# A gate projection moved from behind the first recurrent head to behind all four heads and the rotary key

## The chip, the cores and the metric

One core of a Trainium2 chip runs the whole kernel as one launch. The metric is the device time of one execution in microseconds (us), lower is better. Engines: TensorE (PE, with its weight loads PEld), VectorE (DVE), ScalarE (ACT), GpSimd (POOL), and SyncE (SP), whose queue issues most of the loads.

## The reference, cut to what matters

One transformer-like layer over 512 latent tokens and 256 context tokens, width 1024, all in float32. One input projection feeds multi-head latent attention (4 heads) and a bidirectional gated linear recurrence (HGRN2, 4 heads, 2 directions). The recurrence's output of a head is normalised over its 128 values, scaled, and multiplied by the SiLU of a gate projection `hg`:

```python
    def hgrn_out(o, hg, n):
        o = rmsnorm(o, g_on).astype(hg.dtype).reshape(B, n, HGRN_HEADS * HGRN_VAL_DIM)
        return o * jax.nn.silu(hg)

    lat_out = jnp.concatenate([o_mla_lat, hgrn_out(o_h_lat, hg_l, N)], axis=-1) @ w_out
```

The concatenated head outputs go through `w_out`, a residual with a modulation vector, a second norm, a SwiGLU feed-forward of 2816 columns, and a final norm.

## The kernel before, in words

Every float32 product is split into a high and a low part, and `mm3` (lines 148 to 152) issues three matmuls for it. A weight unit (128x1024) comes in by a load on SP's queue into a `wf` buffer (3 of them), is cast to its high part on ACT (line 132), and its low part is made on DVE (line 133); `wh` and `wl` have 3 buffers each, and `unit(i)` prepares two units ahead. The units are used in the order in which `wi` was packed on the host.

PSUM has two tiles `big` (two banks each) and four tiles `sm` (a bank each).

The order of the stage that the change touches:

- `mla_pass` makes the low-rank query and key inputs, and `mods(6)` and `mods(2)` issue eight `late_mod` sums (line 427: one load of 512 KB and one DVE pass over 128x1024 with a running sum; 32 such sums make the late modulation vectors).
- For each head h: `hgrn_q(h)`, `gates(h, 0)`, `gates(h, 1)`, three projections into a `big` each. After head 0 comes `hg_pass`, the gate projection: it holds both `big` tiles for four units of 24 matmuls, and makes `shg`, the SiLU of the gate, with ACT and DVE (lines 644, 645); between its units it calls `mods(3)`, up to a limit of 12.
- `mla_kpe` projects the rotary key into a `big`, rotates it on DVE, and writes `krh` and `krl`, four ACT casts and four DVE subtractions (lines 726, 727).
- `make_v` (three), `make_qr` (two), `make_q` (four), `make_k(0)`: the attention's values, rotary queries, queries and first keys; then `scores` and the attention (lines 855 to 918); then `wout` (the output projection) with further `mods` in front of it.

The recurrence runs beside this, in generators on the list `side`. `tick()` moves the first three of them on by one step; `project` calls it once or twice in its middle and the main loop calls it after each projection, so that the recurrence's small matmuls stand between projections. `hgrn_dir(h, d)` makes one direction of one head (scan and reciprocal on DVE, transposes, masked scores `pa`, key-value products `kv`, the chain of states `U`). `hgrn_out(h)` waits for both directions and for the gate (`"hg" in done`), sums the two masked score tiles on POOL, makes the head's output in `po` (an `sm`), its norm, the product with `shg` (line 621, four DVE instructions), four transposes (line 627), and `onh`, `onl` (lines 629, 630). For the last head the norm's root is taken with an ACT square root (`fast=last`), and an Exp activation follows it (line 617) so that ACT has Exp's table before the attention. The order on each engine is fixed when the program is built, by a planner that goes by priorities (program order, moved by `prio`) and by its own estimate of when operands are ready.

Of the kernel before, what the change touches and what calls it, by code (L numbers as in the profile page):

```python
# [52 lines left out]
def block_kernel(ctx: ExitStack, tc: tile.TileContext, xT, ctxT, vec, cin, cst, msk, wm, wmt, wi, wqkv, wo, wgu, wd, out):  # L53
# [8 lines left out]
    def nm(s):  # L62
        uid[0] += 1
        return f"{s}_{uid[0]}"
# [4 lines left out]
    def sm():  # L69
        return psum.tile([P, 512], F32, tag="sm", name=nm("sm"), bufs=4)  # L70
# [73 lines left out]
    def unit(i, ahead=2):  # L144
        prefetch(i + 1 + ahead)
        return made[i]
# [320 lines left out]
    HU = 8  # L467

    def gates(h, d):
        ps = project(HU + 3 * h + 1 + d + (4 if h else 0))  # L470
        sg = HG.tile([P, NT], F32, tag="sg", name=nm("sg"), bufs=2)
        nc.scalar.activation(sg, ps[:, :NT], AF.Sigmoid)
        kk = HG.tile([P, NT], F32, tag="kk", name=nm("kk"), bufs=3)
        nc.scalar.activation(kk, ps[:, :NT], AF.Sigmoid, scale=-1.0)
        return sg, kk

    def hgrn_q(h):
        ps = project(HU + 3 * h + (4 if h else 0), ctx_=False)
        q = HG.tile([P, NL], F32, tag="q", name=nm("q"), bufs=2)
        nc.scalar.copy(q, ps[:, :NL])  # L480
        return q
# [106 lines left out]
        dirs[h, d] = (qg, U)  # L588

    def hgrn_out(h):  # L590
        while (h, 0) not in dirs or (h, 1) not in dirs or "hg" not in done:
            yield
        a2 = HG.tile([P, 4, P], F32, tag="a2", name=nm("a2"), bufs=1)
        nc.gpsimd.tensor_add(a2, am[0], am[1])
        for _ in range(3 if h % 2 else 1):
            yield
        po = sm()
        for j in range(4):
            t = po[:, j * P : (j + 1) * P]
            nc.tensor.matmul(t, a2[:, j, :], vt[:, j, h * P : (h + 1) * P], start=True, stop=False,  # L600
                             skip_group_check=True)
            for d in range(2):
                qg, U = dirs[h, d]
                for g in range(2):
                    c = 2 * j + g
                    nc.tensor.matmul(t[g * CH : (g + 1) * CH, :], qg[:, c, :], U[:, c, :], start=False,  # L606
                                     stop=(g == 1 and d == 1), skip_group_check=True, tile_position=(0, g * CH))
        done.add(h)
        sq = HG.tile([P, P], F32, tag="st", name=nm("osq"), bufs=1)
        ss = HG.tile([P, 4], F32, tag="rs_s", name=nm("oss"), bufs=1)  # L610
        for j in range(4):
            nc.scalar.activation(sq, po[:, j * P : (j + 1) * P], AF.Square, accum_out=ss[:, j : j + 1])
        last = h == NH - 1
        with prio(200 if last else 0):
            rr, _ = rstd_cols(HG, (ss, 4), P, fast=last)
        if last:
            nc.scalar.activation(epst2, rr[:, 0:1], AF.Exp, scale=0.0)
        w = HG.tile([P, 4, P], F32, tag="rs_d", name=nm("ow"), bufs=1)
        with prio(200 if last else 0):
            for j in range(4):  # L620
                nc.vector.scalar_tensor_tensor(w[:, j, :], po[:, j * P : (j + 1) * P], rr[:, j : j + 1],
                                               shg[:, j, h * P : (h + 1) * P], op0=ALU.mult, op1=ALU.mult)
        for _ in range(4):
            yield
        pt = sm()
        for j in range(4):
            nc.tensor.transpose(pt[:, j * P : (j + 1) * P], w[:, j, :], ident)
        gon = V("gon")[:, 0:1]
        nc.scalar.activation(onh[:, h, :], pt, AF.Copy, scale=gon)
        nc.vector.scalar_tensor_tensor(onl[:, h, :], pt, gon, onh[:, h, :].bitcast(F32), op0=ALU.mult,  # L630
                                       op1=ALU.subtract)

    def hg_pass():
        acc = [big(), big()]
        acc = [acc[0][:, 0, :], acc[0][:, 1, :], acc[1][:, 0, :], acc[1][:, 1, :]]
        for u in range(4):
            w = unit(HU + 3 + u)
            for tt in range(4):
                for kk in range(2):
                    k = 2 * u + kk  # L640
                    mm3(acc[tt], (hh[:, k, tt * P : (tt + 1) * P], hl[:, k, tt * P : (tt + 1) * P]),
                        sl(w, lambda t: t[:, kk * 512 : kk * 512 + 512]), k == 0, k == KT - 1)
                if u == 3:
                    nc.scalar.activation(shg[:, tt, :], acc[tt], AF.Sigmoid)
                    nc.vector.tensor_mul(shg[:, tt, :], acc[tt], shg[:, tt, :])
                if tt == 1:
                    tick()
            tick()
            mods(3)
        done.add("hg")  # L650

    def mla_pass():
        acc = [big(), big()]
# [72 lines left out]
                nc.scalar.copy(krh[r, c], src)  # L726
                nc.vector.tensor_sub(krl[r, c], src, krh[0:64, c].bitcast(F32))

    KPU = HU + 16
    nm_ = [0]  # L730
    lim_ = [12]

    def mods(n):
        for _ in range(n):
# [6 lines left out]
    for h in range(NH):  # L741
# [6 lines left out]
        side += [hgrn_dir(h, 1, s1, qd), hgrn_out(h)]  # L748
        tick()
        if h == 0:  # L750
            hg_pass()
            mods(12 - nm_[0])
            nc.sync.dma_start(cs[:, CC["cos"][0] :], cst[:, CC["cos"][0] :])
    mla_kpe()
    tick()
    B.release()

    F1 = pool("F1", "right")
# [406 lines left out]
```

## Time and profile before

| | us |
|---|---|
| median of 3 runs | 794.79 |
| lowest, highest run | 792.61, 794.85 |
| profiled execution | 792.44 |
| its span, first to last instruction | 790.6 |

The profiled execution is the one that all rows come from: 1.84 us of its time lie outside the span, and it is 2.35 us under the median. PE is busy for 767.0 us of the span, DVE for 445.0, ACT for 307.2. A wait is shown with the instruction that waited and the one that released it.

### The profile page before, as it was taken

The page shows a single profiled execution, that of the slowest core. Times are in us where ns is not written, and L with a number is a line of the kernel's source. Part 1 is how long each engine was busy: PE and PEld are TensorE (multiplying, and loading weights), DVE is VectorE, ACT ScalarE, POOL GpSimd, SP SyncE. Part 2 cuts the span into 40 slices and gives each one's busy share as a digit, 9 for nine tenths or more (in the row PEclk, how much of TensorE's full clock was granted, in tenths as well). Part 3 has the DMA queues.
Part 4 walks back from the last instruction along what each step waited for, and adds up shares of the span by engine and source line. Part 5 has one row for each costly group of instructions (what it writes and reads, how often), then busy time and mean ns, then how long its engine had stood idle before and what let it go on. Part 6 is the DMA issues. An engine that isn't in the chain of part 4 may idle for free.

```text
span 790.6 us, 10838 instructions
## 1 busy us (share of the span) xinstructions
PE 767.0 (97%) x4342; PEld 630.8 (80%) x4342; DVE 445.0 (56%) x819; ACT 307.2 (39%) x564; POOL 10.1 (1%) x18
## 2 busy tenths in 40 slices
PE   8899999999999989999999999999999999999995
PEld 7568878788887768888999888888888888888885
DVE  4686569739778988984566434432333233223324
ACT  5344245434554576664344223222322222212211
POOL 0000000000000100000000000000000000000000
PEclk8999999999999999999999999999999999999997
DMA  8924723321110022453503354423232333332303
GB/s 326 396 82 142 238 81 107 133 67 61 48 55 28 28 96 98 133 166 148 160 2 107 107 159 133 149 92 107 80 107 82 104 78 96 93 100 82 111 2 107
DMA packets 26708, 88.78 MB, mean 112 GB/s; under 512 B 2977, under 2 KB 5281, under 8 KB 26530
## 3 DMA queue, kind: packets, MB, share of 16 engines
q1 hardware_dynamic: 25570, 87.04, 33.5%
q10 hardware_dynamic: 1088, 1.05, 0.4%
q8 instruction: 34, 0.56, 0.3%
q14 instruction: 16, 0.13, 0.0%
HBM read 85.97 MB, written 2.10 MB: 111 GB/s over the span
## 4 chain that ended last, share of the span: by engine, by line
PE 86%; DVE 7%; DMA 4%; ACT 2%; issue 1%; SPq 0%; DVEq 0%; ACTq 0%
PE big L150 17%; PE big L151 16%; PE big L152 16%; PE sm L150 9%; PE sm L151 9%; PE sm L152 9%; PE big L861 2%; DMA xc<-in_ctxT_dram 1%; PE sm L606 1%; DMA wm<-in_wm_dram 1%; PE big L862 1%; DMA wms<-in_wm_dram 1%; PE sm L880 1%; DVE U L587 1%; PE sm L600 1%
## 5 line engine op out<-in xcount | busy, mean ns | idle before, releaser
L133 DVE TENSOR_TENSOR wl<-wf,wh 128x1024 fp32r<-128x1024 f32 (+2 forms) x100 | 119.6, 1196 | 184.5 <-ACT wh L132 184.3
L132 ACT CAST wh<-wf 128x1024 fp32r<-128x1024 f32 (+2 forms) x100 | 102.9, 1029 | 279.8 <-PE big L151 167.4
L150 PE MATMUL big<-h2h,wh 128*128 128x512 f32 (+1 forms) x368 | 140.3, 381 | 0.0
L151 PE MATMUL big<-h2l,wh 128*128 128x512 f32 (+1 forms) x368 | 140.0, 381 | 0.0
L152 PE MATMUL big<-h2h,wl 128*128 128x512 f32 (+1 forms) x368 | 140.0, 381 | 0.0
L151 PEld LDWEIGHTS big<-h2l,wh 128*128 128x128 f32 x368 | 69.2, 188 | 14.6
L152 PEld LDWEIGHTS big<-h2h,wl 128*128 128x128 f32 x368 | 69.2, 188 | 14.5
L150 PEld LDWEIGHTS big<-h2h,wh 128*128 128x128 f32 x368 | 69.2, 188 | 14.4
L150 PE MATMUL sm<-ah,wh 128*128 128x512 f32 (+1 forms) x198 | 73.5, 371 | 0.0
L152 PE MATMUL sm<-ah,wl 128*128 128x512 f32 (+1 forms) x198 | 73.4, 371 | 0.0
L151 PE MATMUL sm<-al,wh 128*128 128x512 f32 (+1 forms) x198 | 73.4, 370 | 0.0
L427 DVE SCALAR_TENSOR_TENSOR wl<-wl,cs 128x1024 f32<-128x1024 f32 x32 | 39.0, 1220 | 35.0 <-DMA wl<-in_wmt_dram 35.0
L150 PEld LDWEIGHTS sm<-ah,wh 128*128 128x128 f32 x198 | 37.3, 188 | 7.1
L151 PEld LDWEIGHTS sm<-al,wh 128*128 128x128 f32 x198 | 37.3, 188 | 7.1
L152 PEld LDWEIGHTS sm<-ah,wl 128*128 128x128 f32 x198 | 37.3, 188 | 7.1
L150 PE MATMUL big<-hh,wh 128*128 128x512 f32 x104 | 42.8, 411 | 0.0
L150 PE MATMUL big<-wh,hh 128*128 128x512 f32 x96 | 39.4, 414 | 3.3 <-ACT hh L340 1.9
L151 PE MATMUL big<-hl,wh 128*128 128x512 f32 x104 | 40.9, 394 | 0.0
L152 PE MATMUL big<-hh,wl 128*128 128x512 f32 x104 | 40.9, 393 | 0.0
L151 PE MATMUL big<-wl,hh 128*128 128x512 f32 x96 | 38.2, 400 | 0.0
L152 PE MATMUL big<-wh,hl 128*128 128x512 f32 x96 | 38.1, 399 | 0.0
L508 DVE RECIPROCAL G<-S 128x528 f32<-128x528 f32 x8 | 27.5, 3433 | 0.1
(320 smaller groups left out, 1345.9 us busy)
## 6 DMA issues: line engine op xcount, KB each, us to landing
wf<-in_wgu_dram SPq DMA_DIRECT2D x44, 512.0 KB, 3.4
wl<-in_wmt_dram SPq DMA_DIRECT2D x32, 512.0 KB, 3.5
wf<-in_wi_dram SPq DMA_DIRECT2D x25, 512.0 KB, 4.2
wf<-in_wd_dram SPq DMA_DIRECT2D x16, 512.0 KB, 3.5
wms<-in_wm_dram SPq DMA_DIRECT2D x11, 512.0 KB, 9.6
wf<-in_wo_dram SPq DMA_DIRECT2D x8, 512.0 KB, 3.3
wf<-in_wd_dram SPq DMA_DIRECT2D x8, 384.0 KB, 3.1
wm<-in_wm_dram SPq DMA_DIRECT2D x5, 512.0 KB, 10.2
```

Of the source, the lines that this page charges most:

```text
L132: nc.scalar.copy(hi[:, :w], f[:, :w])
L133: nc.vector.tensor_sub(lo[:, :w], f[:, :w], hi[:, :w].bitcast(F32))
L150: nc.tensor.matmul(o, lh, rh, start=start, stop=False, skip_group_check=True)
L151: nc.tensor.matmul(o, lh, rl, start=False, stop=False, skip_group_check=True)
L152: nc.tensor.matmul(o, ll, rh, start=False, stop=stop, skip_group_check=True)
L427: nc.vector.scalar_tensor_tensor(f, f, 1.0, sc, op0=ALU.mult, op1=ALU.mult, accum_out=acc)
L508: nc.vector.reciprocal(I, S)
L587: nc.vector.scalar_tensor_tensor(U[:, c1, :], U[:, c0, :], er[:, 1, c0 : c0 + 1], U[:, c1, :], op0=ALU.mult, op1=ALU.add)
L600: nc.tensor.matmul(t, a2[:, j, :], vt[:, j, h * P : (h + 1) * P], start=True, stop=False, skip_group_check=True)
L606: nc.tensor.matmul(t[g * CH : (g + 1) * CH, :], qg[:, c, :], U[:, c, :], start=False, stop=(g == 1 and d == 1), skip_group_check=True, til ...
L861: nc.tensor.matmul(ps[:, 0, :], L, R[:, :NL], start=(i == 0), stop=(i == 4), skip_group_check=True)
L862: nc.tensor.matmul(ps[:, 1, :NC], L, R[:, NL:], start=(i == 0), stop=(i == 4), skip_group_check=True)
```

## The change

The gate projection `hg_pass` is called after `mla_kpe` instead of after head 0, and its four weight units are packed last in `wi`. `hgrn_out` no longer waits for the gate: it writes the normalised output into the head's own columns of `vt`, the value tile, which no later instruction of that head reads; half of the four writes go to ACT. The new generators `hgrn_fin`, one per head, are put on `side` after the gate pass: they multiply these columns by the gate, one DVE instruction of 128x512, and make the transposes, `onh` and `onl`. The last head's norm is made like the others (three Newton steps on DVE, no square root), the Exp activation moves to the end of `hg_pass`, and the limit of modulation sums before the attention goes from 12 to 8: four sums move into the `mods` calls of the output projection.

```diff
     def hgrn_out(h):
-        while (h, 0) not in dirs or (h, 1) not in dirs or "hg" not in done:
+        while (h, 0) not in dirs or (h, 1) not in dirs:
             yield
...
-        last = h == NH - 1
-        with prio(200 if last else 0):
-            rr, _ = rstd_cols(HG, (ss, 4), P, fast=last)
-        if last:
-            nc.scalar.activation(epst2, rr[:, 0:1], AF.Exp, scale=0.0)
-        w = HG.tile([P, 4, P], F32, tag="rs_d", name=nm("ow"), bufs=1)
-        with prio(200 if last else 0):
-            for j in range(4):
-                nc.vector.scalar_tensor_tensor(w[:, j, :], po[:, j * P : (j + 1) * P], rr[:, j : j + 1],
-                                               shg[:, j, h * P : (h + 1) * P], op0=ALU.mult, op1=ALU.mult)
-        for _ in range(4):
+        rr, _ = rstd_cols(HG, (ss, 4), P)
+        w = vt[:, 0:4, cols]
+        for j in range(4):
+            if j % 2:
+                nc.scalar.activation(w[:, j, :], po[:, j * P : (j + 1) * P], AF.Copy, scale=rr[:, j : j + 1])
+            else:
+                nc.vector.tensor_scalar(w[:, j, :], po[:, j * P : (j + 1) * P], rr[:, j : j + 1], None, op0=ALU.mult)
+        done.add(("n", h))
+
+    def hgrn_fin(h):
+        while ("n", h) not in done:
+            yield
+        w = vt[:, 0:4, h * P : (h + 1) * P]
+        nc.vector.tensor_mul(w, w, shg[:, :, h * P : (h + 1) * P])
+        for _ in range(2):
             yield
         pt = sm()
         for j in range(4):
...
-            mods(3)
-        done.add("hg")
+        nc.scalar.activation(epst2, shg[:, 3, 0:1], AF.Exp, scale=0.0)
+        side.extend(hgrn_fin(h) for h in range(NH))
...
-    lim_ = [12]
+    lim_ = [8]
...
         if h == 0:
-            hg_pass()
-            mods(12 - nm_[0])
+            mods(8 - nm_[0])
             nc.sync.dma_start(cs[:, CC["cos"][0] :], cst[:, CC["cos"][0] :])
     mla_kpe()
     tick()
+    hg_pass()
     B.release()
```

## Rows read from the trace of the kernel before

**Rows 1.** The page, its first part: busy us (share of span) xinstructions.
```profile
PE 767.0 (97%) x4342; PEld 630.8 (80%) x4342; DVE 445.0 (56%) x819; ACT 307.2 (39%) x564; POOL 10.1 (1%) x18
```
**Rows 2.** Stretches: PE, PEld, DVE, ACT, POOL busy (xcount), PE clock, DMA share, GB/s.
```profile
107.30:156.20 48.90, 48.90 (x332) 40.44 (x330) 39.24 (x60) 23.91 (x49) 1.28 (x1) 1.00 0.36 119
156.20:211.40 55.20, 55.20 (x392) 46.60 (x391) 38.02 (x64) 24.30 (x56) 1.28 (x1) 1.00 0.18 58
263.20:296.20 33.00, 29.17 (x187) 21.22 (x185) 30.62 (x60) 22.77 (x47) 3.57 (x4) 1.00 0.21 72
296.20:350.00 53.80, 52.61 (x310) 45.24 (x309) 49.57 (x97) 34.98 (x71) 0.00 (x0) 1.00 0.38 124
350.00:366.00 16.00, 15.13 (x79) 12.47 (x78) 6.19 (x13) 5.68 (x13) 0.00 (x0) 1.00 0.45 165
```
**Rows 3.** Waits of PE, 100 to 300 us: us in total, times, longest us.
```profile
PE big L150 <- DVE krl L727: 1.7, 1, 1.7
...
PE sm L627 <- DVE ow L621: 1.2, 1, 1.2
PE big L150 <- DVE qnl L783: 1.0, 2, 0.7
PE sm L606 <- DVE U L587: 0.6, 1, 0.6
```
**Rows 4.** Timeline of PE at its longest wait: start, duration, instruction [idle before].
```profile
267.91 0.39 PE L152 MATMUL sm<-cq,wl 128*128 128x512 f32 x1
268.14 0.39 PE L150 MATMUL sm<-cq,wh 128*128 128x512 f32 x1
270.19 0.50 PE L150 MATMUL big<-wh,ck 128*128 128x512 f32 x1 [1.67 <-DVE krl L727]
```
**Rows 5.** The gate pass: its matmuls (one group of three) and its DVE product.
```profile
L150 PE MATMUL big<-wh,hh 128*128 128x512 f32 x32 | 13.2, 412 | 0.0
...
L645 DVE TENSOR_TENSOR shg<-big,shg 128x512 f32<-128x512 f32 x4 | 2.8, 689 | 2.7 <-ACT shg L644 2.7
```
**Rows 6.** DVE's groups from 263.2 to 296.2 us: busy us, mean ns | idle before.
```profile
L133 DVE TENSOR_TENSOR wl<-wf,wh 128x1024 fp32r<-128x1024 f32 x4 | 4.9, 1216 | 0.4 <-ACT wh L132 0.4
L810 DVE TENSOR_TENSOR vl<-big,vh 128x512 fp32r<-128x512 f32 x6 | 4.1, 688 | 0.6 <-ACT vh L809 0.6
...
L801 DVE TENSOR_TENSOR qs<-m,qs 64x512 fp32r<-64x512 f32 x4 | 2.7, 686 | 0.1
L783 DVE SCALAR_TENSOR_TENSOR qnl<-big,qnh 128x512 fp32r<-128x512 f32 x4 | 2.7, 684 | 0.3 <-ACT qnh L782 0.3
L630 DVE SCALAR_TENSOR_TENSOR onl<-sm,vc,onh 128x512 fp32r<-128x512 f32 x2 | 1.5, 748 | 0.0
L793 DVE STREAM_SHUFFLE m<-sm 128x512 f32<-128x512 f32 x2 | 1.5, 730 | 0.0
```
**Rows 7.** Timeline of ACT: the last head's table loads among the queries' casts.
```profile
286.72 1.28 ACT L190 ACT_TABLE_LOAD   x1
288.01 0.30 ACT L190 ACTIVATE rsr<-oss,epst 128x4 f32<-128x4 f32 x1
...
292.42 1.28 ACT L617 ACT_TABLE_LOAD   x1
```
**Rows 8.** The late modulation sums: DVE between 296.2 and 350 us.
```profile
L427 DVE SCALAR_TENSOR_TENSOR wl<-wl,cs 128x1024 f32<-128x1024 f32 x12 | 14.6, 1215 | 0.8 <-DMA wl<-in_wmt_dram 0.8
```
**Rows 9.** Issues on SP's queue after the last of these sums' loads.
```profile
346.27 3.86 SPq L122 DMA_DIRECT2D wf<-in_wo_dram  x2
352.38 0.33 SPq L931 DMA_DIRECT2D x<-in_xT_dram  x1
368.69 1.46 SPq L122 DMA_DIRECT2D wf<-in_wo_dram  x2
```
**Rows 10.** Loads by kind: KB each, us from issue to landing.
```profile
wl<-in_wmt_dram SPq DMA_DIRECT2D x32, 512.0 KB, 3.5
wf<-in_wi_dram SPq DMA_DIRECT2D x25, 512.0 KB, 4.2
```

More of the change, by code (lines that the diff above doesn't have):

```diff
@@ L469, in gates @@
     def gates(h, d):
-        ps = project(HU + 3 * h + 1 + d + (4 if h else 0))
+        ps = project(HU + 3 * h + 1 + d)
         sg = HG.tile([P, NT], F32, tag="sg", name=nm("sg"), bufs=2)
@@ L477, in hgrn_q @@
     def hgrn_q(h):
-        ps = project(HU + 3 * h + (4 if h else 0), ctx_=False)
+        ps = project(HU + 3 * h, ctx_=False)
         q = HG.tile([P, NL], F32, tag="q", name=nm("q"), bufs=2)
@@ L597, in hgrn_out @@
         po = sm()
+        cols = slice(h * P, (h + 1) * P)
         for j in range(4):
             t = po[:, j * P : (j + 1) * P]
-            nc.tensor.matmul(t, a2[:, j, :], vt[:, j, h * P : (h + 1) * P], start=True, stop=False,
-                             skip_group_check=True)
+            nc.tensor.matmul(t, a2[:, j, :], vt[:, j, cols], start=True, stop=False, skip_group_check=True)
             for d in range(2):
@@ L636, in hg_pass @@
         for u in range(4):
-            w = unit(HU + 3 + u)
+            w = unit(HU + 13 + u)
             for tt in range(4):
@@ L727, in mla_kpe @@
                 nc.vector.tensor_sub(krl[r, c], src, krh[0:64, c].bitcast(F32))
-    KPU = HU + 16
+    KPU = HU + 12
     nm_ = [0]
-    lim_ = [12]
+    lim_ = [8]
     def mods(n):
@@ L1135 @@
         wi += [tl["hq"][h], tl["ff"][h], tl["fb"][h]]
-        if h == 0:
-            wi += [hg[:, 2 * j : 2 * j + 2].reshape(P, UNIT) for j in range(4)]
     swap = np.arange(64) ^ 16
@@ L1140 @@
     wi += [_tiles(np.concatenate([kp, kp[:, swap]], axis=1))[0]]
+    wi += [hg[:, 2 * j : 2 * j + 2].reshape(P, UNIT) for j in range(4)]
     arr["wi"] = ct(np.stack(wi))
```

## Prediction

> **What bounds the kernel now.** I read the page's busy shares first, then the busy time by stretches, then PE's own waits, and last the timelines around them. PE is busy for 97% of the span [rows 1], and its granted clock is full in every stretch that the change touches [rows 2]. The change takes away no matmul, so PE's busy time cannot shrink; only PE's idle time can. So the question is where PE idles and what ends that.
>
> From head 0's gates to the end of head 2's projections PE is never idle: 48.90 of 48.90 us and 55.20 of 55.20 [rows 2]. In the stretch from 263.2 to 296.2, between the rotary key and the first scores, PE is busy for 29.17 of 33.00 us while DVE is busy for 30.62: DVE sets the pace there [rows 2]. The waits say the same. PE waits 1.7 us for `krl` (the rotary key's last reads of its `big` tile), 1.2 for the last head's gated output `ow`, 1.0 in two pieces for `qnl`, and, a little earlier, 0.6 for the chain `U` in front of head 2's output [rows 3]. Then comes the attention, where PE is busy for 52.61 of 53.80 us and DVE for 49.57: close to both limits [rows 2].
>
> A wait costs a little more than its idle time. In a filled queue a matmul of 512 columns starts 0.23 us after the one before (267.91 to 268.14); at the `krl` wait the next start is 2.05 us later, so 1.82 us are lost where the idle time shown is 1.67 [rows 4]. I add 0.15 for each restart: the three waits for `krl`, `ow` and `qnl` (four pieces, 1.7 + 1.2 + 1.0 = 3.9 idle) are worth 3.9 + 4 x 0.15 = 4.5 us. That is the most this stretch can give back.
>
> **The change part by part.** *The gate pass.* It is 4 units x 4 token tiles x 2 x 3 = 96 matmuls, 32 of each of three kinds [rows 5], at 0.23 us [rows 4]: 22.1 us of PE. It asks for little of DVE: four products at 0.69 [rows 5] and four weight units' low parts at 1.22 [rows 6], 2.8 + 4.9 = 7.7 us. Put behind the rotary key it gives DVE 22.1 - 7.7 = 14.4 us to catch up on the `krl` chain, the last `U` chain and the last head's norm. Its four loads of 512 KB now stand in SP's queue behind the rotary key's weights; they land in 4.2 us [rows 10] and a unit of the pass lasts 22.1 / 4 = 5.5 us with two units prepared ahead, so they cost nothing.
>
> *Where it was.* Before, it stood between heads 0 and 1. If it had been DVE's only relief there, taking it away would show. In the 104.1 us from 107.3 to 211.4 DVE is busy for 39.24 + 38.02 = 77.3 [rows 2]; the pass takes away 22.1 us of PE and 2.8 + 4.9 of DVE, and the four modulation sums 4 x 1.22 = 4.9 more, at the price of [rows 8]. That leaves 64.7 of DVE in 82.0 of PE, 79%. So the heads can stand back to back: zero, covered by that slack. What changes is head 0's output: it now follows its `U` chain by one step, as head 2's output does, and head 2 paid 0.6 us idle for that [rows 3]. I charge 0.7 for head 0 (bounds 0 and 1.5, twice that row).
>
> *The `krl` wait.* The gate pass holds two `big` tiles, and the second is the one that `krl` must release. Two token tiles of the first unit, 12 matmuls or 2.8 us, can run in front of it, where now a wait of 1.67 us stands after a few matmuls pulled forward. I keep 0.5 of the 1.82 (bounds 0 and 1.82).
>
> *Behind the gate pass.* Here the late work collects. PE: values, rotary queries and queries are 36 + 12 + 24 = 72 wide matmuls, 16.6 us; the first keys 6 wide and 6 half as wide, 2.1; 16 transposes, taken at half of 0.23, 1.8: together 20.5. DVE: `vl` 4.1; three weight units 3.7; rotary queries 1.5 (shuffle) + 2.7 (`qs`) + six of the width of `qnl` 4.1 = 8.3; `qnl` 2.7; four `onl` at 0.75, 3.0 [rows 6]; four gate products of 128x512 at 0.69, 2.8 [rows 5]; `knl` about 1.1, as one of the width of `vl` and one smaller: together 25.7. So DVE has 5.2 us more to do than PE. But the first scores don't wait for the rotary queries of heads 2 and 3 (4.1) nor for the last `onl` (0.75), which can run into the attention. That leaves 0.3 as the lower bound and 5.2 as the upper; I take 1.0, near the lower end, because ACT leaves this stretch too: the square root's and the Exp's table loads, 1.28 us each, stand in its queue there now [rows 7], and one Exp load at the end of the gate pass replaces them. The trace has the square root starting right where its load ends (288.01 after 286.72 + 1.28) [rows 7]. The Trainium skill, "ScalarE: Activation LUTs", section "What ACT_TABLE_LOAD costs", counts a drain of about 1.38 us on top of each load; by it the pair would cost 5.3 us and the new load 2.7 instead of 2.6 and 1.3, and the sum would gain another 1.4. These rows show no such gap.
>
> *The norm.* The four products with the gate become two DVE and two ACT writes of the same size per head, and the last head's norm trades a square root for more small DVE steps: it now runs under the gate pass's matmuls. Nothing; without that cover some 2 us.
>
> *The four modulation sums.* They move to the output projection's `mods`, but the planner already pulls such sums into the attention: 12 of them lie between 296.2 and 350, 14.6 us of DVE [rows 8], one each 53.8 / 12 = 4.5 us. Four more at that pace end 18 us later, about where the stretch from 350 to 366 ends, where DVE is busy for 6.19 of 16.00 us [rows 2]. Their loads (3.5 us each [rows 10]) go ahead of two weight units of the output projection, issued from 346.27, and past the load of `x`, at 352.38; the next issue is at 368.69 [rows 9], so SP's queue has some 16 us of room and what waits behind is not due sooner. I take 0; the upper bound is all four in the attention, 4 x 1.22 = 4.9 us.
>
> *Sum.* -4.5 + 0.5 + 1.0 + 0.7 = -2.3 us against the profiled execution: 792.44 - 2.3 = 790.1. The median stands 2.35 above the profiled execution; on it the sum gives 794.79 - 2.3 = **792.5 us**.
>
> **The rivals.** *A: full cover.* Nothing remains of the waits: no rest at `krl`, none behind the gate pass, head 0's output ready in time, and head 2's 0.6 (0.7 with its restart) gone as DVE has less to do per head: -4.5 - 0.7 = -5.2, 789.6. For it: DVE's 14.4 us of relief. Against it: DVE's 25.7 us on PE's 20.5 behind the pass.
>
> *B: no change.* The waits move instead of going: the lag behind the gate pass reaches 3 us, in place of 1.0, as ACT's casts feed DVE one by one, and head 0's output takes its 0.7; -4.5 + 0.5 + 3 + 0.7 = -0.3, 794.5. For it: rows in which DVE is the slower engine right there, and an attention near both limits. PE's matmuls stay as they are. The Trainium skill, "Perfetto Trace Analysis", section "Identifying the Most-Contended Engine", says to optimise the engine of highest occupancy first; this change leaves the work of PE, that engine here at 97%, as it is, and by that rule it would move nothing.
>
> *C: slower.* DVE becomes the bound from the end of the gate pass to the end of the attention, with the four sums inside: 25.7 us behind the pass, 49.57 in the attention [rows 2] and 4 x 1.22 = 4.9 [rows 8] make 80.2, against 20.5 + 52.61 = 73.1 of PE. The difference is 7.1; 1.2 of it is idle time of PE that the attention has already (53.80 - 52.61), so 5.9 are new, in place of the forecast's 1.0: -4.5 + 0.5 + 0.7 + 5.9 = +2.6, 797.4. It decides from a new lag of 5.7 (then the sum is the 2.4 that the measurement can tell). For it: 12 sums are in the attention already, on a DVE that is 92% busy. Against it: at the pace of rows 8 the four come after the attention, and without them the new lag is 1.0.
>
> **How the numbers follow.** About 0.3% (2.4 us) can be told from no change. The forecast has 0.41, spread from -4.0 to -0.8 with a little more than half beyond -2.4; A 0.17; B 0.22; C 0.20. Faster: 0.24 + 0.17 = 0.41. Same: 0.17 + 0.22 = 0.39. Slower: 0.20. The forecast's own range is 790.8 to 794.0. The range takes in A, with 1.0 below it for shorter waits in the attention, and C, with 0.6 above it: 788.6 to 798.0; beyond stand the upper bounds taken together.
>
> **What would show each step.** Right: a gate pass of some 22 us behind the rotary key with PE busy throughout; the wait for `krl` at 0.5 or under; no square root on ACT before the attention; head 0's output with a wait for `U` of some 0.6; between the gate pass and the first scores some 21.5 us with DVE nearly always busy; the last sums after the attention. Wrong: PE idle between heads 0 and 1 (then the pass had been cover there); waits for `qnl`, `krl` or the transposes' input of over 3 us behind the pass (B); more than 13 sums inside the attention and longer waits for `ptl` or the exponentials there (C). A different interleaving by the planner of the recurrence's small matmuls could move any of these by a microsecond, which is the weakest part of this forecast.

## The result and the profile after

The changed kernel takes 796.4 us (median of 15 runs, 792.84 to 799.26) beside 794.97 for the kernel before on the same chip (15 runs, 792.31 to 796.38): ratio 1.003, 95% interval 1.0016 to 1.0044. It is 1.3 to 3.5 us slower, where 2.3 us faster was forecast.

**How the times are compared below.** The profiled execution has a span of 797.4 us, the one of before 790.6, and 4.5 of these 6.8 us lie in code that both share: the first query projection starts at 101.58 us before and at 106.11 after. The windows of the start show why; first the kernel before, then the changed one (columns: stretch, length, busy time of PE, PEld, DVE, ACT, POOL, PE's granted clock, DMA share, GB/s):

```profile
10.00:20.00 10.00, 7.84 (x55) 5.50 (x53) 5.14 (x17) 4.51 (x8) 0.00 (x0) 0.68 1.03 414
20.00:30.00 10.00, 9.34 (x60) 5.56 (x56) 6.50 (x16) 3.85 (x9) 0.00 (x0) 0.98 1.03 408
```

```profile
10.00:20.00 10.00, 7.54 (x50) 5.76 (x52) 4.45 (x16) 4.59 (x8) 0.00 (x0) 0.66 1.03 415
20.00:30.00 10.00, 9.42 (x40) 4.77 (x34) 4.88 (x9) 3.01 (x7) 0.00 (x0) 0.50 1.02 407
```

From 20 to 30 us TensorE ran at nearly full clock in the one execution and at its lower level, 1.2 GHz, in the other. Every timed execution has its mean granted clock, and time follows it closely: one line through all 344 executions of this study (20 kernels, one level for each, one slope for all) gives 0.68 us for each 0.001 of mean clock and leaves a scatter of 0.55 us, where the runs of one kernel spread over 3 to 10 us. So I give, beside each measured ratio, the kernel's level at equal clock (0.987) against the kernel before, good to 0.3 us with 11 or more runs and to 0.5 with six. It is a fit to the runs, not a separate measurement. For the changed kernel it says +1.6 us. It is fair only where the clock fell in code that the kernels share; four runs, named behind the table below, have a fall of their own.

The traces, one execution each, are taken from mark to mark and so without the start; they say +2.3. From the first query projection to the first scores the kernel before takes 194.62 us and the changed one 196.91; from there to the output projection's first matmul with the attention's output 69.47 and 69.43. By these marks all of the loss lies ahead of the first scores. But the two do not have the same work there (the same columns, from mark to mark, before and changed):

```profile
101.58:296.19 194.61, 189.98 (x1360) 154.64 (x1361) 155.71 (x305) 98.02 (x225) 7.61 (x7) 1.00 0.22 71
106.11:303.01 196.90, 190.99 (x1368) 155.75 (x1368) 151.27 (x298) 99.11 (x231) 8.33 (x7) 1.00 0.17 54
```

The eight further matmuls are the rest of head 1's keys, two of 512 columns and six of 256, some 1.2 us; the kernel before issues them behind its first scores. So about half of the 2.3 is where the mark falls, and the sum over both stretches is the one to trust.

PE's own waits in the changed kernel, from 104 to 372 us (waiting matmul, what it waited for, us in total, times, longest), to be read beside [rows 3]:

```profile
PE sm L606 <- DVE U L587: 2.6, 3, 1.2
PE big L150 <- DVE krl L731: 1.5, 1, 1.5
PE big L865 <- DVE knl L780: 1.5, 1, 1.5
...
PE big L865 <- ACT knh L779: 1.0, 1, 1.0
PE big L865 <- ACT pp L871: 1.0, 1, 1.0
PE sm L150 <- DVE ptl L887: 0.7, 1, 0.7
PE sm L551 <- ACT cT L542: 0.4, 1, 0.4
PE sm L631 <- DVE vt L626: 0.4, 1, 0.4
```

The waits for `ow` and `qnl` are gone. The one for `krl` is not, the one for `U` has gone from 0.6 to 2.6, and the first keys, `knh` and `knl`, are new with 2.5.

The windows of the gate pass, of the stretch behind it and of the attention, which answer to [rows 2]:

```profile
247.50:278.00 30.50, 28.96 (x159) 22.08 (x155) 17.62 (x38) 12.31 (x31) 3.70 (x4) 1.00 0.20 61
278.00:303.00 25.00, 23.64 (x112) 18.62 (x112) 22.94 (x36) 17.17 (x27) 0.00 (x0) 1.00 0.22 70
303.00:363.00 60.00, 56.78 (x333) 48.73 (x333) 55.01 (x106) 39.69 (x81) 0.00 (x0) 1.00 0.42 132
```

Under the gate pass DVE has room, 17.62 us of 30.50; behind it DVE is busy for 22.94 of 25.00.

**The `krl` wait.** PE and DVE of the changed kernel there (timelines: start, us, engine, line, operation, tiles, and in brackets the idle time and what ended it):

```profile
247.53 0.50 PE L150 MATMUL big<-wh,hh 128*128 128x512 f32 x1
...
252.39 0.40 PE L151 MATMUL big<-wl,hh 128*128 128x512 f32 x1
254.30 0.47 PE L150 MATMUL big<-wh,hh 128*128 128x512 f32 x1 [1.51 <-DVE krl L731]
```

```profile
247.90 0.67 DVE L724 TENSOR_TENSOR kp<-big,cs 64x512 f32<-64x512 f32 x1
...
249.97 1.77 DVE L133 TENSOR_TENSOR wl<-wf,wh 128x1024 fp32r<-128x1024 f32 x1
251.66 0.67 DVE L727 TENSOR_TENSOR kp<-kp,kpm 64x512 f32<-64x512 f32 x1
...
253.74 0.42 DVE L731 TENSOR_TENSOR krl<-big,krh 64x256 fp32r<-64x256 f32 x1
```

The twelve matmuls of the gate pass that were to run in front did so, from 247.53 to 250.43. But DVE reads the rotary key's tile last at 253.74, behind a weight's low part and two of the rotary key's own steps that don't read that tile. That low part took 0.55 us longer than others of its shape (see the last section).

**The first scores.** DVE, ACT and PE in front of them:

```profile
300.02 1.22 DVE L133 TENSOR_TENSOR wl<-wf,wh 128x1024 fp32r<-128x1024 f32 x1
...
302.17 1.39 DVE L805 TENSOR_TENSOR qs<-m,qs 64x512 fp32r<-64x512 f32 x2
303.59 1.23 DVE L133 TENSOR_TENSOR wl<-wf,wh 128x1024 fp32r<-128x1024 f32 x1
304.73 1.95 DVE L780 TENSOR_TENSOR knl<-sm,knh 128x512 fp32r<-128x512 f32 x4
```

```profile
299.54 1.26 ACT L804 CAST qs<-m 64x512 fp32r<-64x512 f32 x2 [0.48 <-DVE m L800]
300.82 0.60 ACT L786 ACTIVATE qnh<-big 128x512 fp32r<-128x512 f32 x1
301.44 1.05 ACT L132 CAST wh<-wf 128x1024 fp32r<-128x1024 f32 x1
302.39 1.62 ACT L779 CAST knh<-sm 128x512 fp32r<-128x512 f32 x4
```

```profile
303.02 0.73 PE L865 MATMUL big<-knh,qnh 128*128 128x512 f32 x2 [1.02 <-ACT knh L779]
...
305.47 0.73 PE L865 MATMUL big<-knl,qnh 128*128 128x512 f32 x2 [1.48 <-DVE knl L780]
```

The keys' high parts stand behind the rotary queries' casts, which wait for DVE; the low parts stand behind the rotary queries' differences and the low part of a weight for a later stage.

**Table loads.** No square root is left ahead of the attention; one load for Exp stands at the end of the gate pass, and its activation starts where the load ends:

```profile
279.56 1.28 ACT L653 ACT_TABLE_LOAD   x1
280.86 0.20 ACT L653 ACTIVATE epst<-shg 128x1 f32<-128x1 f32 x1
```

By the Trainium skill, "ScalarE: Activation LUTs", section "What ACT_TABLE_LOAD costs", a drain of about 1.38 us comes on top; as in [rows 7], these rows show none.

### The profile page after: what moved, and what is told of

Read it like the earlier page. It is cut to its first block, busy times and chain, and to the rows that moved or that the text cites. A ratio compares the mean times of both kernels' runs of the same rounds, so it can differ in the third digit from the quotient of the medians.

```text
span 797.4 us, 10848 instructions
## 1 busy us (share of the span) xinstructions
PE 771.0 (97%) x4342; PEld 633.3 (79%) x4342; DVE 447.7 (56%) x822; ACT 308.7 (39%) x570; POOL 10.8 (1%) x18
## 4 chain that ended last, share of the span: by engine, by line
PE 88%; DVE 7%; ACT 3%; issue 1%; DMA 1%; SPq 0%; DVEq 0%; ACTq 0%
PE big L150 17%; PE big L151 17%; PE big L152 16%; PE sm L150 9%; PE sm L151 9%; PE sm L152 9%; PE big L865 2%; PE sm L606 1%; PE sm L884 1%; PE sm L320 1%; PE big L866 1%; DMA xs<-in_xT_dram 1%; PE sm L601 1%; DVE wl L133 1%; ACT wh L132 1%
## 5 line engine op out<-in xcount | busy, mean ns | idle before, releaser
L150 PEld LDWEIGHTS big<-wh,hh 128*128 128x128 f32 x96 | 18.3, 193 | 14.1 <-issue 5.0
```

Of the source, the lines that this page charges most:

```text
L150: nc.tensor.matmul(o, lh, rh, start=start, stop=False, skip_group_check=True)
```

## The experiments

My theory, before the runs: three places lose, and each by the order of queues, not by a lack of room (the even heads' output one step behind its `U` chain; the rotary key's reads; the keys behind the rotary queries). The rivals were that DVE has too much work wherever it stands, and that the place of the gate pass itself costs.

All times of this section, with the ratio to the kernel before on the same chip; "level" is that at equal clock, and "trace" the time of the profiled execution from the first query projection to the output projection's first matmul with the attention's output, both in us against the kernel before (the changed kernel: +1.6 and +2.3):

| run | median us | ratio, 95% interval | level | trace |
|---|---|---|---|---|
| e1 three steps | 793.46 | 0.9990 (0.9962 to 1.0017) | -1.1 | -0.7 |
| e2 reads first | 794.73 | 1.0006 (0.9980 to 1.0031) | +0.3 | +0.4 |
| e3 Silu on ACT | 797.33 | 1.0029 (1.0009 to 1.0048) | +1.1 | +1.6 |
| e4 gate pass early | 804.44 | 1.0113 (1.0088 to 1.0138) | +5.9 | +8.5 |
| e5 = e1 and e2 | 793.76 | 1.0002 (0.9981 to 1.0023) | -0.8 | -0.5 |
| e6 rotary queries first | 797.98 | 1.0052 (1.0030 to 1.0074) | +2.7 | +2.7 |
| e7 = e5 and e6 | 794.87 | 1.0008 (0.9989 to 1.0027) | +0.1 | -0.1 |
| e8 before, sums late | 792.98 | 0.9998 (0.9976 to 1.0020) | -0.1 | 0.0 |
| e9 = e7 and Silu | 793.66 | 0.9994 (0.9975 to 1.0014) | -1.0 | -0.8 |
| e10 before, reads first | 793.14 | 0.9987 (0.9968 to 1.0006) | -0.7 | -0.9 |
| e11 chain first | 796.61 | 1.0035 (1.0016 to 1.0053) | +0.8 | +2.5 |
| e12 = e9, no gate products | 792.63 | 0.9984 (0.9964 to 1.0004) | -2.1 | -2.0 |
| e13 = e5, program order | 790.97 | 0.9958 (0.9941 to 0.9976) | -2.6 | -2.8 |
| e14 = e13 and Silu | 789.69 | 0.9934 (0.9911 to 0.9956) | -3.3 | -3.5 |
| e15 = e5 and Silu | 793.55 | 0.9987 (0.9970 to 1.0004) | -1.8 | -1.1 |
| e16 = e15, no gate products | 793.08 | 0.9984 (0.9960 to 1.0008) | -2.8 | -2.4 |
| e17 before, mended order | 799.32 | 1.0075 (1.0054 to 1.0095) | +2.1 | +7.2 |
| e18 = e17 and Silu | 801.01 | 1.0090 (1.0062 to 1.0119) | +1.9 | +6.4 |

Level and trace lie within 0.7 us of each other in all but four runs: e4, e11, e17 and e18. In their traces the granted clock falls again, to 1.2 GHz, inside the stretch that the edits touch. In e4 (three windows), e17 (two) and e18 that comes at long waits of the kernel's own, told below:

```profile
294.00:298.00 4.00, 0.00 (x0) 0.00 (x0) 3.91 (x9) 1.64 (x2) 0.00 (x0) 1.00 0.00 0
298.00:304.00 6.00, 2.38 (x6) 1.96 (x7) 3.60 (x11) 0.73 (x2) 0.00 (x0) 0.51 0.55 175
304.00:310.00 6.00, 6.00 (x33) 5.00 (x32) 3.48 (x8) 1.45 (x3) 0.00 (x0) 0.92 0.24 87
```

```profile
284.00:288.00 4.00, 4.00 (x12) 2.66 (x11) 3.90 (x9) 2.01 (x4) 0.00 (x0) 0.65 0.41 131
295.00:302.00 7.00, 4.61 (x17) 4.07 (x17) 4.25 (x13) 2.38 (x5) 0.00 (x0) 0.53 0.26 75
```

The lower clock is there a cost of the edit, and the level, which takes it out, is too kind: for these three the ratio (about +9, +6 and +7 us) and the trace are the ones to read. In e11 the fall comes at the waits for the first keys, which the changed kernel has as well, without a fall; whether it belongs to e11 is open.

**The `U` chains: e1 and e11.** e1:

```diff
-        for _ in range(3 if h % 2 else 1):
+        for _ in range(3):
```

> The even heads' output gets three steps behind its U chain instead of one, as the odd heads' has. Theory: in the changed kernel PE loses 1.35 us at head 0's output and 0.48 + 1.38 at head 2's, because the output's matmuls come one step behind a chain of seven additions that stands behind the next direction's work in DVE's queue; with three steps the waits for U (2.6 us idle) fall under 0.8, the stretch from the first query projection to the first scores shrinks from 196.9 to about 194.3 us, and the time falls by 2 to 3 us, to the kernel before or a little below it. Rival: DVE is simply late in the heads without the gate pass between them; then the idle time moves to the gates or to the next chain, and stretch and time stay within 0.7 us of the changed kernel.

The gain is 2.7 us at equal clock. PE's wait for `U` in e1:

```profile
PE sm L606 <- DVE U L587: 0.8, 1, 0.8
```

The wait for `krl` is no longer in the list either: with the outputs later, the order around the rotary key changed by itself, and 0.7 us is lost at one set of key-value products (line 578) instead. e11 leaves the one step and moves the chain ahead on DVE:

```diff
-        with prio(-100):
+        with prio(0):
             U = HG.tile([P, NCH, P], F32, tag="U", name=nm("U"), bufs=2)
```

> The changed kernel, with the U chain's seven additions no longer set back by 100 in the order, so that they stand ahead of the next direction's work on DVE; the even heads' output keeps its one step. Theory: head 0's and head 2's losses (1.35, 0.48 and 1.38 us) come from the chain's place in DVE's queue, so they fall under 1.0 in sum and the time falls by 1.5 to 2.5 us at equal clock, nearly as with three steps. Rival: the chain is late because its inputs are (ACT's copies of PSUM, the matmuls that make them), one step is too little in any order; then the waits for U stay at 2 us or more, and the next direction's gates are later too: the time is the same or up to 2 us longer.

By the level only 0.8 us is gained; the trace, up to the first scores, is 1.0 shorter. The loss at head 0 falls from 1.35 to 0.72, but the one at head 2 stays (1.87), and PE now waits 0.8 for a step of a norm (`rst`). So the chain's place in DVE's queue is a part of it; that one step is too little is the larger part, as the rival had it.

**The rotary key: e2 and e5.** e2 reads the tile first, with precedence (the added lines; those that they replace are left out):

```diff
+        def split(src, c):
+            for r in (slice(0, 64), slice(64, 128)):
+                nc.scalar.copy(krh[r, c], src)
+                nc.vector.tensor_sub(krl[r, c], src, krh[0:64, c].bitcast(F32))
+        with prio(400):
+            split(ps[0:64, NL:NT], slice(NL, NT))
+            nc.vector.tensor_mul(kp[0:64, :], ps[0:64, :NL], C("cos")[0:64, :])
+            nc.vector.tensor_mul(kp[64:128, :], ps[64:128, :NL], C("sin")[64:128, :])
+        nc.scalar.copy(m[0:64, :], kp[64:128, :])
+        nc.vector.tensor_add(kp[0:64, :], kp[0:64, :], m[0:64, :])
+        split(kp[0:64, :], slice(0, NL))
```

> The rotary key's reads of its PSUM tile (two copies, two differences, two products) are put ahead of its other steps and given precedence in the queues. Theory: PE's wait for krl (1.5 us idle, 1.67 lost) is the order of ACT and DVE behind the rotary key's matmuls, not a lack of room; with the reads first the tile comes free some 3 us earlier than the 7.5 us it takes now, the wait is gone, and the stretch from the first query projection to the first scores shrinks by 1.5 us. Rival: the delayed steps (the last head's chain and its sum) only come later, the last head's output becomes later by as much, and the stretch stays the same within 0.5 us.

PE no longer waits for `krl`, the stretch to the first scores shrinks from 196.91 to 195.06, and 1.3 us is gained: the theory held. e5 puts e1 and e2 together.

> Three steps for every head's output and the rotary key's PSUM reads first, together. At equal granted clock the two alone were 2.7 and 1.3 us under the changed kernel. Theory: they are different waits of PE, at different places, so they add: 4.0 us under the changed kernel and 2.4 under the kernel before at equal clock, near 792.5 where that stands at 794.9. Rival: both free DVE for the same late work, the rotary key's wait is shorter by itself once the outputs stand later, and the sum is no better than 3 us under the changed kernel.

The rival was right: 2.4 us under the changed kernel, no more than e1 alone, since e1 had already moved the `krl` wait away.

**The place of the gate pass: e4.** The pass goes back behind head 0, and its units to their old place in `wi`; the rest of the change stays (cut; the two lines added behind `mla_kpe` go out of `hg_pass`):

```diff
         if h == 0:
+            hg_pass()
             mods(8 - nm_[0])
...
     mla_kpe()
+    nc.scalar.activation(epst2, shg[:, 3, 0:1], AF.Exp, scale=0.0)
+    side.extend(hgrn_fin(h) for h in range(NH))
     tick()
-    hg_pass()
```

> The gate pass goes back between heads 0 and 1, with its weights' place in the queue; all else of the change stays (normalised outputs in the value columns, gate multiplied at the end, four modulation sums late, Exp's table behind the rotary key). Theory: it is the place of the pass that costs: head 0's wait for U (1.35 us) goes, and so does what collects behind the pass; but the rotary key's wait stays at 1.7, and the end's gate products now wait for the last head's norm without cover: the stretch from the first query projection to the first scores is 194.5 to 196, about 1.5 us below the changed kernel and like the kernel before within 1 us. Rival: the place is neutral and the rewritten outputs cost (products and transposes at the end); then the stretch stays at 196.9 within 0.5 us or gets longer.

The theory fell: the trace is 6.3 us longer than the changed kernel's. The rival's longer stretch came (203.2 us to the first scores), but not its reason, a place that is neutral. Head 0's loss does go (0.3 is left), and no wait for `krl` shows but one of 1.7 for `vl`; but the transposes now wait for the last head's product with the gate:

```profile
PE sm L631 <- DVE vt L626: 7.9, 1, 7.9
```

The last head's norm, a dozen small DVE steps and its products, has nothing to run under. Two low parts of weights (2.4 us) stand among its steps, as the change gave up the precedence that this norm had; how much of the 7.9 that makes was not tried. For the outputs as the change writes them, the place behind the heads is the better one by far.

**The sums alone: e8.** The kernel before, with only the limits changed:

```diff
-    lim_ = [12]
+    lim_ = [8]
-            mods(12 - nm_[0])
+            mods(8 - nm_[0])
```

> The kernel before with one part of the change alone: the four modulation sums behind the gate pass move to the output projection. Theory: neutral, within 0.5 us of the kernel before at equal clock, since the planner draws some 12 sums into the attention in either case. Rival: the sums are what the changed kernel pays for: DVE and the loads behind them are short in the attention or the output projection, and this kernel is 1.5 us slower than the one before, all of the difference found.

-0.1 us: neutral, as forecast.

**Behind the gate pass: order against work.** e3 takes four products off DVE:

```diff
-                    nc.scalar.activation(shg[:, tt, :], acc[tt], AF.Sigmoid)
-                    nc.vector.tensor_mul(shg[:, tt, :], acc[tt], shg[:, tt, :])
+                    nc.scalar.activation(shg[:, tt, :], acc[tt], AF.Silu)
```

> The gate is written by ACT in one step (Silu instead of Sigmoid, then a product on DVE): four DVE products of 0.69 us fall away at the gate pass's end. Theory: the loss of some 4 us around the first scores (waits for knh, knl and pp) comes from DVE, which is behind from the gate pass on; 2.8 us less DVE there shorten it by 1.5 to 2.5 us, and the time falls by as much. Rival: the queue of ACT sets it, with casts that feed DVE one by one; then nothing is gained, and a further table load of 1.28 us may cost up to 1 us more.

0.5 us is gained, nearer to the rival. e6 changes the order, not the work:

```diff
-        with prio(-100):
+        with prio(100):
             nc.vector.stream_shuffle(m2, ps, SWAP)
```

> The changed kernel, with the rotary queries' steps given precedence (by 100) where they had the opposite. Theory: the loss of 1.2 + 1.6 us before the first scores is not DVE's sum of work but its order: the last rotary query holds the buffers in which head 0's keys are to be written, and behind it a weight's low part stands ahead of knl; with the rotary queries early the waits for knh and knl fall from 2.5 to under 0.8 us idle and the stretch from the first query projection to the first scores shrinks by some 2 us. Rival: DVE has 5 us more to do than PE there, whatever its order; then another wait takes the place (qnl, vt or pp), and the time stays within 0.7 us of the changed kernel at equal clock.

My theory of the order, as I had put it, fell: 1.1 us worse. The waits for the first keys are gone, but others stand in their place, as the rival said (its 0.7 was too little):

```profile
PE big L150 <- DVE vl L814: 1.2, 1, 1.2
PE big L865 <- DVE qnl L787: 1.2, 1, 1.2
```

The rotary queries now hold up the values, whose `big` tiles PE needs. With e5 in it, e7 tells the same (0.9 worse than e5):

> Three steps for every output, the rotary key's reads first and the rotary queries first, together. Theory: three separate places of wrong order; together 6 us under the changed kernel at equal clock, 4 to 4.5 under the kernel before. Rival: DVE is the bound from the gate pass to the end of the attention; the third edit then adds less than 0.7 to the other two, as the attention's waits grow by what the stretch before it gains.

e9 adds Silu to e7, and e12 leaves out the final products with the gate as well, as e16 does for e15:

```diff
-        nc.vector.tensor_mul(w, w, shg[:, :, h * P : (h + 1) * P])
```

e9:

> All three reorderings, and the gate written by ACT in one step (Silu), which takes 2.8 us of products from DVE around the end of the gate pass. Theory: behind the gate pass DVE's sum of work is the limit (it is busy for 20.7 of 22.0 us in the stretch from the gate pass's end to the first scores, with every order tried the loss there stays near 3 us); with DVE's products gone 1.5 to 2.5 us of the waits for vl, qnl and vt go, and the kernel stands 1.5 to 2.5 us under the one before at equal clock. Rival: a chain of single latencies (PE, then a cast on ACT, then a difference on DVE) sets the pace, not a sum; then less than 0.8 us is gained on the same kernel without Silu.

e12:

> As the one with less DVE work, and the four products with the gate at the end are left out altogether, so the outputs go on ungated (that part of the computation is missing): 5.6 us less DVE work than in the changed kernel from the gate pass on, and the transposes no longer wait for a product. Theory: DVE's sum is the limit behind the gate pass; the loss between the gate pass and the first scores falls under 1.0 us, and the kernel stands 2.5 to 4 us under the one before at equal clock. Rival: single latencies set the pace; the loss there stays at 2 us or more, and only the wait for vt (0.5) is gone.

Each 2.8 us less of DVE gives about 1.1 us (+0.1, -1.0, -2.1), and in e9 PE waits 2.6 us in one piece for `vl`, behind ten steps of the rotary queries. Neither theory comes out clean: the work counts for four tenths of itself, and a large wait stays. So order was tried again, with the rotary queries between the values and the queries, where the program has them:

```diff
-        with prio(-100):
+        with prio(0):
             nc.vector.stream_shuffle(m2, ps, SWAP)
```

e13:

> Three steps, reads first, and the rotary queries' steps in program order: behind the values' low parts, ahead of the queries (neither put back nor ahead by 100). If DVE's order is what loses the 3 us behind the gate pass, this order, which makes neither head 0's keys nor the values wait, loses under 1.5 us there, and the kernel stands 2 to 3 us under the kernel before at equal clock. If DVE's sum of work is the limit, another wait takes the place (qnl or pp), the loss stays near 3 us and the time within 0.7 us of the two reorderings alone (0.8 under before).

e14:

> As the one in program order, with the gate written by ACT in one step (2.8 us less on DVE). If sum and order both count, the loss behind the gate pass falls under 0.8 us and the kernel stands 3 to 4 us under before at equal clock, the best of all. If order alone counts, it equals the one in program order within 0.5 us. If latencies set the pace, both stay within 1 us of the two reorderings alone.

e15:

> Three steps and reads first, the rotary queries last as in the changed kernel, and the gate in one step on ACT. On the changed kernel that step gained 0.5 us. If order is the limit, the waits for knh and knl stay at 2.5 us idle and no more than 0.6 us is gained over the two reorderings alone; if the sum, 1.5 us or more.

e16:

> As the one before in this list, and without the four products with the gate (the outputs go on ungated: that part of the computation is missing): 5.6 us less on DVE, the rotary queries still last. If the order is the limit, knh and knl still wait for the last rotary query and a weight's low part, 2 us idle or more, and only the 0.5 us at the transposes is gone; if the sum, under 1 us of loss is left between the gate pass and the first scores, and the kernel stands 3 us under before at equal clock.

At the first keys the order decides. With the same work on DVE, e13 stands 1.8 us under e5, as its theory had it. In e13, from 104 to 312 us, of the waits behind the gate pass these are left:

```profile
PE big L869 <- DVE knl L784: 0.7, 1, 0.7
...
PE big L869 <- ACT pp L875: 0.4, 1, 0.4
...
PE sm L631 <- DVE vt L626: 0.4, 1, 0.4
```

In e16, with 5.6 us less on DVE but the first order, the keys are still waited for, 2.3 us in all:

```profile
PE big L867 <- DVE knl L782: 1.5, 1, 1.5
PE big L867 <- ACT pp L873: 1.0, 1, 1.0
PE big L867 <- ACT knh L781: 0.8, 1, 0.8
```

But less work on DVE helps beside that, 0.5 to 1.1 us for each 2.8 in all three orders (the changed kernel to e3, e5 to e15 to e16, e7 to e9 to e12, e13 to e14), though at the keys it hardly shows; where that part is gained was not traced. So e15 (1.0 gained) lies between its two theories, and e16 has the waits that the order foretold with nearly the time that the sum foretold. e14's level is as forecast, but not its waits: 1.1 us is left for `knl`.

e14 beats both kernels: 789.69 us, 0.66% under the kernel before (interval 0.44 to 0.89%), and 4.9 us under the changed kernel at equal clock.

**Is it the move or the mended order? e10, e17, e18.** e10 is the kernel before with the reads of e2.

> The kernel before, its gate pass in place, with the rotary key's PSUM reads first as the only edit. Theory: the krl wait is a matter of order alone, and no move of the gate pass is needed for it: the 1.8 us lost there go, the waits for ow and qnl behind it stay, and the time falls by 1.0 to 1.8 us at equal clock. Rival: DVE sets the pace from the rotary key to the first scores in that kernel; then what krl gives back is lost again at ow or qnl, and the time stays within 0.5 us.

-0.7 us: in between. The wait for `krl` becomes one of 0.6 for `kp`, and that for `ow` 0.3, but `qnl` (1.5 in all), `knl` (0.9) and `onl` (0.8) take up most of the gain. e17 gives the kernel before all three reorderings, e18 Silu too.

> The kernel before, gate pass in its old place, with the three reorderings of the changed kernel's best order (three steps for every output, the rotary key's reads first, rotary queries in program order). Theory: the moved pass is what gives DVE room, so without it the last head's chain, its norm and the late work still collide: no more than 1.2 us under the kernel before at equal clock, and the move is worth 1.4 us or more. Rival: the order was all; then this kernel stands 2.6 us under before as the changed one does, and the move is worth nothing.

> As the one before in this list, with the gate in one step on ACT (2.8 us less DVE, between heads 0 and 1). Theory: DVE has slack there (PE never waits in that stretch), so nothing more is gained: within 0.5 us of the one without. Rival: DVE's work is short everywhere in the heads; then 0.8 us or more is gained, as in the changed kernel.

The same order that takes 0.42% off with the changed kernel (e13) adds 0.75% to the kernel before (e17), 6.0 us. In e17 PE waits at the end of the recurrence:

```profile
PE sm L627 <- DVE ow L621: 5.6, 1, 5.6
PE big L150 <- DVE qnl L787: 2.4, 1, 2.4
```

On DVE the last steps of the last head's `U` chain now stand among the rotary queries' steps:

```profile
284.25 0.34 DVE L587 SCALAR_TENSOR_TENSOR U<-U,er 128x128 f32<-128x128 f32 x1
...
285.22 1.41 DVE L805 TENSOR_TENSOR qs<-m,qs 64x512 fp32r<-64x512 f32 x2
286.66 0.35 DVE L587 SCALAR_TENSOR_TENSOR U<-U,er 128x128 f32<-128x128 f32 x1
...
287.53 0.34 DVE L587 SCALAR_TENSOR_TENSOR U<-U,er 128x128 f32<-128x128 f32 x1
```

The last head's norm begins at 293.45, beside 286.25 in the kernel before. Silu gives nothing measurable there (the level is 0.2 lower, the median 1.7 higher). So it is the changed kernel, the moved pass with the outputs written for it, that lets that order pay; the move was not tried without the new outputs. These edits were made for the changed kernel: which of them harms the kernel before was not tried, nor whether that kernel has an order of its own that does as well as e14.

## Why the prediction was wrong

The steps that failed are the lag behind the gate pass, put at 1.0 where 3.35 us were lost, the rest at `krl`, put at 0.5 where it was 1.67, and head 2's output, for which the sum had no term and which lost 1.13 more than before. Of the waits that the move was to remove, those for `ow` and `qnl` went, but more came up elsewhere, at places where the order of the queues made PE wait. By PE's losses from start to start, as the prediction counted them, step by step:

- **The three waits, -4.5.** Right in size for `ow` and `qnl`, which lost 2.64 us before and nothing after.
- **The rest at `krl`, 0.5.** Failed: 1.67 is lost, of 1.82 before, inside the bounds (0 to 1.82) but at their far end. The prediction set the twelve matmuls of the gate pass against "a few matmuls pulled forward". Those few, a token tile of the values and four matmuls of rotary queries, were 10 x 0.23 = 2.3 us of cover, and the move takes them away. The new cover, those twelve and two more, 3.2 us, replaced the old. e2 shows that the order of the reads was the cause, not the cover.
- **The lag behind the gate pass, 1.0.** The largest error. PE loses 0.53 at the transposes (`vt`), 1.18 at `knh` and 1.64 at `knl`: 3.35, inside the bounds (0.3 to 5.2). The reason given for the lower end was that the first scores don't wait for the rotary queries of heads 2 and 3. They need none of it, but the planner had put those steps, and a weight of the next stage, ahead of the first keys in both queues. The stretch from the pass to the first scores, told as some 21.5 us, took 25.0 (277.99 to 303.02): 2.1 us of it, by the paces of 0.23 and 0.12, are head 1's keys, which the prediction's sum for PE left out. e13 shows that the order makes most of this, and e16 that taking work away leaves most of it.
- **Head 0's output, 0.7.** Mechanism right, size off: 1.35, inside the bounds (0 to 1.5). What was missed is head 2: taking out the pass and rewriting the outputs also changed its order, and its loss went from 0.73 to 0.48 + 1.38 us. e1 takes most of both back.
- **The sums, 0.** Right (e8, where they move in the kernel before). 13 stand between the first scores and the output projection's first matmul with the attention's output, where 12 did, not 16, and that stretch is no longer, so rival C, whose 797.4 lies near the result, is not what happened.
- **The norm, nothing, "without that cover some 2 us".** Nothing is right; without the cover PE waits 7.9 (e4), the low parts among its steps included.
- **The table loads.** Right.

With these, up to the output projection: -2.64 - 0.15 (`krl`) + 0.53 + 1.18 + 1.64 + 1.35 + 1.13 (head 2) = +3.0. The other waits behind the first scores are 0.6 shorter (2.68 before, 2.04 after, from start to start), which leaves +2.4, and the marks show 2.3. Ahead of the first scores it is +1.4 by these steps; head 1's keys, some 1.2 us, stand on that side too, and the attention, which has them no longer, makes up for the 1.64 at `knl`.

Rival B had the right idea, that waits move instead of going, and its lag of 3 was close; it left head 2 out and had the same 0.5 at `krl`. The idea behind the forecast, that the pass is better cover behind the heads than between them, is borne out by e4 for the outputs as the change writes them, and e13 beside e17 points the same way; the change as written did not collect it. The rule of the Trainium skill, "Perfetto Trace Analysis", section "Identifying the Most-Contended Engine", to work on the most contended engine first, does not say that such a change moves nothing, as the prediction took it: that engine is PE here, and e14, 0.66% faster, shortens PE's waits with its matmuls untouched.

## What to carry to other kernels

A block of matmuls that needs little of the other engines is cover wherever it stands: when it moves, list what it covered in its old place and what it pushes out of its new one, and count only the difference. The steps that "can run later" only do so if the queue has them later: look up what stands ahead of the first thing that the next stage needs, on each engine, and price that. After a move, priorities that were set for the old order are worth another look: here three small edits of the order turned 1.6 us of loss into 2.6 us of gain. And before times are compared at equal clock, look where the clock fell: a fall that a kernel's own wait brings belongs to that kernel's time.

## What the runs showed of the hardware

- The lower clock of the start differs from run to run: from 20 to 30 us the granted clock was 0.98, 0.50 and 1.00 in three profiled executions (before, changed, e13), after PE had been busy for 7.84, 7.54 and 6.61 of the 10 us ahead at 0.68, 0.66 and 0.83; the first query projection then started at 101.58, 106.11 and 100.42. It moves a run by more than the whole change.
- Inside the kernel the clock fell at PE's long waits: in e4 PE stood idle for 7.9 us until 301.62 and the granted clock was 0.51 from 298 to 304, though PE was busy again from 301.62 on; in e17 it was 0.53 from 295 to 302, at a wait of 5.6 us, and 0.65 from 284 to 288, behind one of 2.4. The mean clocks of these two and e18, 0.982 to 0.984 over their runs, are the lowest of the study.
- The low part of a weight at 249.97, shown above, took 1.77 us, where the other 95 of that shape in the same trace took 1.22 to 1.23; it overlapped with an addition on POOL (249.36 to 250.66). In e3, e6 and e11 the same step, again over that addition, took 1.77 as well. In e2, where a low part overlaps with that addition too, it kept its 1.21 us, and the addition took 2.56 us beside 1.30 in the changed kernel. What decides which of the two is longer was not tested.
